# Two-block transformer on one core: 32-slot experts with contiguous weights, other key and output steps in the recurrence, a pre-normed half-step

## The chip, the cores and the metric

One core of one Trainium2 chip runs the whole program. The metric is the device time of one execution in microseconds (us), as the median of the runs. The engines go by the profile's short names: PE is TensorE's matmul (PEld its weight load), DVE is VectorE, ACT is ScalarE, POOL is GpSimd and SP is SyncE, which issues nearly all DMAs here.

## The reference

All is float32, batch 1, width 1024. The first block is a gated feed-forward half-step on 272 tokens, a hybrid attention mixer and a second half-step. The second block has two layers over 256 latent and 256 context tokens: layer 0 has a gMLP mixer, layer 1 a bidirectional recurrence, and each ends with a mixture of 32 experts, two per token (layer 0 on 512 tokens, layer 1 on the 256 latents).

```python
def swiglu(x, w_gate, w_up, w_down):
    return (jax.nn.silu(x @ w_gate) * (x @ w_up)) @ w_down

def _wkv_step(S, inp):                       # one token of the recurrence
    r_t, w_t, k_t, v_t, a_t, b_t = inp
    sa = jnp.einsum('zbhvk,zbhk->zbhv', S, a_t)
    S = S * w_t[..., None, :] + sa[..., :, None] * b_t[..., None, :] + v_t[..., :, None] * k_t[..., None, :]
    return S, jnp.einsum('zbhvk,zbhk->zbhv', S, r_t)

def hier_moe(h, ...):
    ...
    top_logit, top_idx = lax.top_k(exp_logits, TOP_K)           # 2 of the chosen group's experts
    weights = (p_grp * jax.nn.softmax(top_logit, axis=-1)).astype(h.dtype)
    ...
    def expert_block(args):
        xb, e = args
        return (jax.nn.silu(xb @ w_gate[e]) * (xb @ w_up[e])) @ w_down[e]
```

The context's recurrence only makes the state with which that of the latents starts, in both directions.

## The kernel before

Activations lie feature-major: 128 features on the partitions, eight chunks of them, tokens along the free axis. Nothing is kept in lower precision. A product that has to be exact is done by `mm3` (L1098) as three single-pass products of two-part operands; `wpart` (L1077) and `split` make the parts, the high one on ACT, the low one on DVE. Weights come through a ring of buffers of 2 MB (`wbuf`, `wtile`, `more_ring`); their DMAs all stand in SP's queue, in the order of their use. The order of the instructions on each engine is set by the framework's scheduler from the program's order and its own timing model, not by hand.

*First half-step* (`ffn`, L328). The squares of the input are summed over features by products with ones (L304) into `r`, 1/sqrt of the mean square. The products run on the input that is only scaled by the gain (L335); `r` is multiplied into both products as they leave PSUM (L350, L351). The modulation vectors of both layers are made beside (`ada`, L593: 32 stationary columns, four column groups of PE in turn), so that its 2 KB rows and the half-step's weights alternate in SP's queue.

*Experts* (`moe`, `experts`, L983). Assignments are sorted into 64 slots per expert; two experts make a pass of 128 slots, so there are 16 passes per layer. A pass loads two gate and two up tiles of 2 MB (`wtile`, L282) and two buffers of down weights, each from two DMAs of 1 MB (L1011). In PE's columns 0 to 63 one expert runs, in 64 to 127 the other:

```python
for b, p in ((0, pg), (1, pu)):
    for k in range(KD):
        for j in range(2):
            nc.tensor.matmul(p[64 * j:64 * j + 64], X[:, k, 64 * j:64 * j + 64], W[2 * b + j][:, k], start=(k == 0), ...
```

These are the records of L998; L1017 is the down product, L921 and L927 gather the next pass's tokens, L963 and L966 add a pass's result to the residual stream. In DRAM a weight's row of 512 or 1024 floats is what lies together: 2 KB of it go to one partition at a time. Assignments beyond the 64 slots would be done after the passes in a loop of extra blocks (`extra`), whose count SP and the other engines load from `xinfo` (L1033). Layer 1's ring has eight buffers: two from before the layer and six opened at its start.

*Recurrence* (`rwkv`). It runs as eight units of four heads, four of the context and then four of the latents, each in both directions z and in four chunks of 64 tokens. A unit has stages that are put beside those of its neighbours:
- `unit_keys` (L1308): decays (`ts` L1344 and L1346, their running sum L1348, exponentials `W` and `Wi` L1350, L1351), keys (L1358, L1359), receptances (L1362), removal vectors and added keys `BX` (L1366 to L1371), and their products (L1382, masked on the way out at L1383, L1386 and L1389);
- `unit_inverse` (L1558): a triangular inverse; its 16-token blocks are solved row by row by 30 small DVE operations that depend on each other (L1592, L1593);
- `unit_values`, then `unit_steps` (L1412): for each chunk T (L1447), U (L1458), the next state (L1473, L1478, with `hs` by POOL at L1466), and for the latents the output, in which a product with 128 rows (L1487) and one with 64 (L1488) alternate:

```python
for z in range(2):
    ...
    for mm in range(NM):
        for hh in range(2):
            mmul(p[o, cs], CL[mm][1][:, hh, z, s], HV[:, hh, mm * 2 + z], start=True, stop=False, ...)
            mmul(p[o, cs], un.LBr[half(z), mm * 2 + hh, s], UV[half(z), z, cs], start=False, stop=True, ...)
```

The functions that the change touches follow with the profile's line numbers.

## Time and profile before

| | us |
|---|---|
| median of 3 runs | 2869.97 (2868.59 to 2870.29) |
| span of the profiled execution | 2864.8 |
| difference to the median | 5.2 |
| PE busy | 2589.3 (90% of the span) |
| DVE busy | 1491.7 (52%) |
| ACT busy | 933.0 (33%) |
| POOL busy | 314.4 (11%) |
| DMA | 616.64 MB, mean 215 GB/s |

The page gives the profiled execution's span and no other time of it. The shares are averages over stages. In order of time these are the first half-step, the mixer and the second half-step, then gMLP, the experts of layer 0 (about 1057 to 1607 us), the recurrence's projections, its units (about 1772 to 2311) and layer 1's experts (to the end). In the lines of groups "busy" is the sum over the records of a group and "mean ns" the duration of one; matmuls overlap each other, so a group's busy time can be less than count times mean. An f32 matmul of this program leaves two records.

### The profile page before, as it was taken

What the parts mean: (1) busy time and instruction counts of PE and PEld (TensorE: products, weight loads), DVE (VectorE), ACT (ScalarE), POOL (GpSimd) and SP (SyncE); (2) the same over time, 40 slices, a digit from 0 to 9 for tenths busy, and PEclk for the clock granted to TensorE, in tenths of its full rate; (3) what the DMA queues carried; (4) which work ended last, traced back from release to release, by engine and by line L of the source; (5) the groups of instructions that cost most, each with busy time, mean ns of one, the idle gap of its engine ahead of it and who ended that gap; (6) DMA issues with size and microseconds to landing.
All of it is one profiled execution on the core that took longest, in us unless ns stands there. A gap on an engine that the chain in (4) does not pass through costs nothing. (4 is left out here: it accounts for less than half of the span.)

```text
span 2864.8 us, 43441 instructions
## 1 busy us (share of the span) xinstructions
PE 2589.3 (90%) x17524; PEld 1719.8 (60%) x17524; DVE 1491.7 (52%) x3267; ACT 933.0 (33%) x1686; POOL 314.4 (11%) x460
## 2 busy tenths in 40 slices
PE   8998999998999979999999597787799979999987
PEld 7986757997788744433333286666677744333332
DVE  5644855664564453443333686988975452222222
ACT  4433654543442231111110354554443222111111
POOL 0000100000100000000000212556552000000000
PEclk9999979999999989999999799887676879999999
DMA  8688801543222159999999333221111459999996
GB/s 282 239 318 288 288 15 54 212 171 128 99 89 88 45 194 384 370 363 365 362 367 364 103 114 115 64 69 40 35 45 27 136 203 387 386 387 387 386 386 254
DMA packets 339235, 616.64 MB, mean 215 GB/s; under 512 B 29059, under 2 KB 77779, under 8 KB 336467
## 3 DMA queue, kind: packets, MB, share of 16 engines
q1 hardware_dynamic: 337040, 609.66, 59.4%
q10 hardware_dynamic: 1926, 4.13, 0.4%
q8 instruction: 141, 2.31, 0.3%
q14 instruction: 64, 0.52, 0.1%
q0 software_dynamic: 64, 0.02, 0.0%
HBM read 604.15 MB, written 9.60 MB: 214 GB/s over the span
## 5 line engine op out<-in xcount | busy, mean ns | idle before, releaser
L998 PE MATMUL pg<-w,X 128*64 128x512 f32 x2048 | 510.1, 598 | 12.7 <-DMA w<-in_moe_up_dram 9.8
L1083 DVE TENSOR_TENSOR wl<-w,wh 128x1024 fp32r<-128x1024 f32 (+2 forms) x208 | 248.9, 1200 | 166.9 <-ACT wh L1082 165.1
L998 PEld LDWEIGHTS pg<-w,X 128*64 128x64 f32 x2048 | 154.0, 137 | 301.3 <-issue 281.8
L1082 ACT ACTIVATE wh<-w 128x1024 fp32r<-128x1024 f32 (+2 forms) x208 | 215.4, 1040 | 351.2 <-PE ps L1102 259.7
L966 DVE SCALAR_TENSOR_TENSOR Rl<-pc,mods,Rl 128x256 f32<-128x256 f32 x256 | 118.3, 480 | 298.0 <-PE pc L963 296.2
L1017 PE MATMUL py<-w,hT 128*64 128x512 f32 x992 | 231.6, 602 | 7.2 <-ACT hT L954 4.5
L1101 PE MATMUL ps<-xs,wh 128*128 128x272 f32 (+1 forms) x704 | 202.5, 288 | 3.5 <-ACT wh L1082 3.5
L1103 PE MATMUL ps<-xs,wl 128*128 128x272 f32 (+1 forms) x704 | 201.4, 288 | 1.4 <-DVE wl L1083 1.4
L1102 PE MATMUL ps<-xs,wh 128*128 128x272 f32 (+1 forms) x704 | 201.2, 286 | 0.0
L963 PE MATMUL pc<-tk,y 128*128 128x512 f32 (+1 forms) x512 | 139.6, 376 | 17.2 <-DVE Rl L966 8.0
L963 PEld LDWEIGHTS pc<-tk,y 128*128 128x128 f32 x512 | 77.6, 188 | 125.4 <-issue 72.9
L1017 PEld LDWEIGHTS py<-w,hT 128*64 128x64 f32 x992 | 67.4, 137 | 130.5 <-issue 115.1
L949 DVE SCALAR_TENSOR_TENSOR hh<-hh,tw,pg 128x512 f32<-128x512 f32 x32 | 23.9, 747 | 231.7 <-PE pg L998 231.7
L1101 PEld LDWEIGHTS ps<-xs,wh 128*128 128x128 f32 x704 | 134.0, 190 | 8.4 <-ACT wh L1082 4.7
L1103 PEld LDWEIGHTS ps<-xs,wl 128*128 128x128 f32 x704 | 133.4, 190 | 4.4 <-issue 2.5
L1102 PEld LDWEIGHTS ps<-xs,wh 128*128 128x128 f32 x704 | 133.8, 190 | 0.1
L976 ACT ACTIVATE y<-py 128x512 fp32r<-128x512 f32 x62 | 37.0, 597 | 279.1 <-PE py L1017 237.9
L977 DVE TENSOR_TENSOR y<-py,y 128x512 fp32r<-128x512 f32 x62 | 42.6, 687 | 136.8 <-ACT y L976 136.8
L928 ACT ACTIVATE X<-px 128x512 f32<-128x512 f32 x64 | 35.4, 596 | 228.0 <-PE pg L998 214.8
L948 ACT ACTIVATE hh<-pg 128x512 f32<-128x512 f32 x32 | 19.1, 598 | 254.6 <-PE pg L998 254.6
L1102 PE MATMUL ps<-hid,wh 128*128 128x272 f32 (+1 forms) x352 | 100.1, 284 | 0.0
L1103 PE MATMUL ps<-hid,wl 128*128 128x272 f32 (+1 forms) x352 | 100.0, 284 | 0.0
(492 smaller groups left out, 5528.7 us busy)
## 6 DMA issues: line engine op xcount, KB each, us to landing
w<-in_moe_gate_dram SPq DMA_DIRECT2D x64, 2048.0 KB, 9.4
w<-in_moe_up_dram SPq DMA_DIRECT2D x64, 2048.0 KB, 19.7
w<-in_moe_down_dram SPq DMA_DIRECT2D x128, 1024.0 KB, 14.4
w<-in_ada_w_dram SPq DMA_DIRECT2D x24, 2048.0 KB, 9.3
w<-in_w_down_dram SPq DMA_DIRECT2D x16, 1408.0 KB, 6.7
w<-in_w_gate_dram SPq DMA_DIRECT2D x8, 2048.0 KB, 9.0
w<-in_w_up_dram SPq DMA_DIRECT2D x8, 2048.0 KB, 7.8
w<-in_ga_w_in_dram SPq DMA_DIRECT2D x8, 2048.0 KB, 10.7
```

What stands on the lines that cost most here:

```text
L928: nc.scalar.activation(X[:, b * 4:(b + 1) * 4].rearrange("p k s -> p (k s)"), p[:, :4 * width], AF.Copy)
L963: nc.tensor.matmul(p[:, :n], y[j][:rows, k * 128:(k + 1) * 128], o, start=(j == 0), stop=(j == 1))
L966: nc.vector.scalar_tensor_tensor(R[t][:, k], p[:, s], self.mod(l, 5, k, t), R[t][:, k], op0=OP.mult, op1=OP.add)
L976: nc.scalar.activation(y[0][:rows, s], p[:rows], AF.Copy)
L977: nc.vector.tensor_tensor(y[1][:rows, s], p[:rows], y[0][:rows, s], op=OP.subtract)
L998: nc.tensor.matmul(p[64 * j:64 * j + 64], X[:, k, 64 * j:64 * j + 64], W[2 * b + j][:, k], start=(k == 0), stop=(k == KD - 1), skip_group_ ...
L1017: nc.tensor.matmul(p[64 * j:64 * j + 64], hT[:, k, 64 * j:64 * j + 64], Wd[b][:, j, k], start=(k == 0), stop=(k == 3), skip_group_check=True)
L1082: self.nc.scalar.activation(hi, view, AF.Copy)
L1083: self.nc.vector.tensor_tensor(lo, view, hi, op=OP.subtract)
L1101: mm(p, w[0], x[1], start=start, stop=False, skip_group_check=True)
L1102: mm(p, w[0], x[0], start=False, stop=False, skip_group_check=True)
L1103: mm(p, w[1], x[0], start=False, stop=stop, skip_group_check=True)
```

## The change

Eight things are changed together.
- The expert weights are laid out by the host so that a tile's part for one partition is contiguous: 16 KB for gate and up, 8 KB for down, which is loaded for two experts by one DMA of 2 MB.
- Layer 1 has 32 slots per expert, so four experts make a pass and there are eight passes; layer 0 keeps 64.
- Layer 1's six ring buffers are allocated after the layer's other tiles.
- `unit_keys` makes decays that start with a column of ones (`W1`, four tiles that live as long as the units), `Wi` for both halves of `BX` in one tile with a single buffer, and `BX` as (scaled ta on ACT) times key (DVE for the removal vectors, POOL for the added keys), then one product of 512 columns with `Wi`; the copies, `b0` and the separate addition of 1 on DVE are gone.
- `unit_inverse` does the row solve of every other unit on POOL.
- `unit_steps` issues the output products of the latents by shape.
- `ffn` norms the input of the first half-step before the products.
- The three parts of an exact product are issued small first in the first half-step and the mixer (as everywhere before), large first elsewhere. The router's logits take tokens as the stationary operand and come out token-major, without transposes.

```diff
-CAP = 64
-LIM = 64
+CAPS = (64, 32)
...
+LARGE_FIRST, SMALL_FIRST = ((0, 0), (0, 1), (1, 0)), ((0, 1), (0, 0), (1, 0))
...
-    for n in ("gate", "up", "down"):
-        a["moe_" + n] = f[f"moe_w_{n}_2"]
+    for n in ("gate", "up"):
+        a["moe_" + n] = f[f"moe_w_{n}_2"].reshape(2, NE, KD, 128, 512).transpose(0, 1, 3, 2, 4).reshape(2, NE, 128, 4096)
+    a["moe_down"] = f["moe_w_down_2"].reshape(2, NE, 4, 128, 2, 512).transpose(0, 1, 4, 3, 2, 5).reshape(2, NE, 2, 128, 2048)
...
-                nc.vector.tensor_scalar(x, h[:, k], self.v(g, k), None, op0=OP.mult)
+                if normed:
+                    nc.vector.scalar_tensor_tensor(x, h[:, k], self.v(g, k), r[:, :n], op0=OP.mult, op1=OP.mult)
+                else:
+                    nc.vector.tensor_scalar(x, h[:, k], self.v(g, k), None, op0=OP.mult)
...
+                    if normed:
+                        nc.scalar.activation(sg, pg[:, :n], AF.Silu)
+                        nc.vector.tensor_mul(sg, sg, pu[:, :n])
...
             pool = es.enter_context(self.tc.tile_pool(name=self.uid("moe"), bufs=1))
+            if l:
+                es.enter_context(self.more_ring(6, before=self.rings))
...
-                        nc.tensor.matmul(p[r, :SEQ], wr[:, k], h[:, k, t * SEQ:(t + 1) * SEQ], start=(k < 2), stop=(k >= KD - 2), skip_group_check=True)
-                    lp = rt.tile([128, SEQ], F32, tag="lp", name=self.uid("lp"), bufs=2)
-                    nc.scalar.activation(lp, p[:, :SEQ], AF.Copy)
...
+                        for j in range(2):
+                            c = t * SEQ + j * 128
+                            nc.tensor.matmul(p[j][:, :36], h[:, k, c:c + 128], wr[:, k, :36], start=(k == 0), stop=(k == KD - 1))
...
-                W = [self.wtile(s[2 * q + j], KD, 512) for s in (gate, up) for j in range(2)]
...
+                W = [[self.wtile(s[G * q + j], KD, 512) for j in range(G)] for s in (gate, up)]
+                for w, p in zip(W, (pg, pu)):
                     for k in range(KD):
...
+                        for j in range(G):
+                            a = slice(cap * j, cap * j + cap)
+                            nc.tensor.matmul(p[a], X[:, k, a], w[j][:, k], start=(k == 0), stop=(k == KD - 1), skip_group_check=True)
...
+                    for j in range(G * q, G * q + G, 2):
+                        t = self.wbuf()
+                        nc.sync.dma_start(t.rearrange("p (j x) -> p j x", j=2), down[j:j + 2, b].rearrange("j p x -> p j x"))
...
-        mm(p, w[0], x[1], start=start, stop=False, skip_group_check=True)
-        mm(p, w[0], x[0], start=False, stop=False, skip_group_check=True)
...
-                v.tensor_scalar(ts, ts, 1.0, None, op0=OP.add)
+                nc.scalar.activation(ts, ts, AF.Identity, bias=un.W1[z][:, 0, 0:1])
+
+                BX = un.BX[mm, z] = un.near("BX", [128, 4, 2, C], 4)
+                nc.scalar.activation(BX[:, :, z], un.chunks(ta), AF.Identity, bias=self.eps[:, 4:5], scale=-0.5)
+                nc.scalar.activation(BX[:, :, 1 - z], un.chunks(ta)[:, :, back], AF.Identity, bias=un.ka[:, 1, m:m + 1], scale=un.ka[:, 0, m:m + 1])
...
+                Wp, Wi = un.W1[z], un.near("Wi", [128, 4, 2, C], 1)
...
-                    v.tensor_mul(q[:, :, 1:], knv[o, :, 1:], Wv[o, :, :C - 1])
-                    v.tensor_copy(q[:, :, 0:1], knv[o, :, 0:1])
+                    v.tensor_mul(un.CL[mm][0][o, hh, z], knv[o], Wx[o])
...
-                v.scalar_tensor_tensor(b0, ta, 1.0, f(kn), op0=OP.add, op1=OP.mult)
-                v.scalar_tensor_tensor(BX[:, :, z], un.chunks(b0), -0.5, un.chunks(Wi), op0=OP.mult, op1=OP.mult)
...
-                g.tensor_tensor(t1, t1, f(k), op=OP.mult)
...
-                v.tensor_mul(BX[:, :, 1 - z], un.chunks(t1)[:, :, back], un.chunks(Wi)[:, :, back])
...
+                v.tensor_mul(BX[:, :, z], BX[:, :, z], knv)
+                g.tensor_tensor(BX[:, :, 1 - z], BX[:, :, 1 - z], un.chunks(k)[:, d], op=OP.mult)
...
+                v.tensor_mul(BX.rearrange("p c a t -> p (c a t)"), BX.rearrange("p c a t -> p (c a t)"), Wi.rearrange("p c a t -> p (c a t)"))
...
-                            mmul(p[o, cs], CL[mm][1][:, hh, z, s], HV[:, hh, mm * 2 + z], start=True, stop=False, skip_group_check=True)
-                            mmul(p[o, cs], un.LBr[half(z), mm * 2 + hh, s], UV[half(z), z, cs], start=False, stop=True, skip_group_check=True)
...
+                        for z in range(2):
+                            mmul(p[z][at[z][0], cs], CL[mm][1][:, hh, z, s], HV[:, hh, mm * 2 + z], start=mm + hh == 0, stop=False, skip_group_check=True)
+                for n in range(NM * 2):
+                    cs = slice(n * 64, (n + 1) * 64)
+                    for z in range(2):
+                        mmul(p[z][at[z][0], cs], un.LBr[half(z), n, s], UV[half(z), z, cs], start=False, stop=n == NM * 2 - 1, skip_group_check=True)
...
-            v.tensor_tensor(tv, Ls[:, s, s + 1:].unsqueeze(2).to_broadcast([128, n, s + 1]), Xs[:, s:s + 1, :s + 1].to_broadcast([128, n, s + 1]), op=OP.mult)
-            v.tensor_tensor(Xs[:, s + 1:, :s + 1], Xs[:, s + 1:, :s + 1], tv, op=OP.add)
...
+            e2.tensor_tensor(tv, Ls[:, s, s + 1:].unsqueeze(2).to_broadcast([128, n, s + 1]), Xs[:, s:s + 1, :s + 1].to_broadcast([128, n, s + 1]), op=OP.mult)
+            e2.tensor_tensor(Xs[:, s + 1:, :s + 1], Xs[:, s + 1:, :s + 1], tv, op=OP.add)
```

The order on three engines shows what the scheduler makes of it. The first place is PE in a step of the latents' units, the output products of one direction; `pt` is their PSUM tile, `HV` the state and the values, `UV` the step's result, `u` the unit's keys and receptances, `pi` and `pk` are products of a neighbouring unit. Before:

```order
L1487 MATMUL pt_17632<-HV_17555,u_16523 64x64
L1624 MATMUL pi_17953<-Xd_17813,LBc_17242 32x32 x22
L1382 MATMUL pk_18244<-u_18034,BX_18235 128x128 x4
L1382 MATMUL pk_18254<-u_18035,BX_18235 128x128 x4
L1473 MATMUL ph_17620<-UV_17586,u_16760 64x64 x2
L1488 MATMUL pt_17632<-UV_17586,u_16520 64x64
L1487 MATMUL pt_17632<-HV_17555,u_16523 64x64
L1488 MATMUL pt_17632<-UV_17586,u_16520 64x64
L1487 MATMUL pt_17632<-HV_17555,u_16525 64x64
L1488 MATMUL pt_17632<-UV_17586,u_16520 64x64
```

The changed program at the same step of the same unit, with line numbers of the changed file (L1506 is the product with 128 rows, L1510 that with 64):

```order
L1506 MATMUL pt_17481<-HV_17404,u_16396 64x64 x2
L1506 MATMUL pt_17481<-HV_17404,u_16398 64x64 x2
L1636 MATMUL pi_17733<-G_17664,XT_17663 32x32 x52
L1492 MATMUL ph_17469<-UV_17435,u_16621 64x64 x2
L1510 MATMUL pt_17481<-UV_17435,u_16393 64x64 x4
L1636 MATMUL pi_17733<-G_17664,XT_17663 32x32 x3
```

The program writes the two directions in turn, one tile each; the scheduler issues the four products of one shape and one tile together and those of the other direction later, as here in most steps.

The second place is the row solve of the seventh unit, which stands in POOL's queue in the changed program, with `hs` of a running unit's step (L1485) and the keys of the decayed values (L1425) in the same queue:

```order
L1614 TENSOR_TENSOR tp_18439<-Ls_18437,Xs_18438 128x55
L1615 TENSOR_TENSOR Xs_18438<-Xs_18438,tp_18439 128x5x11
L1447 COPY HV_18186<-Hst_13895 64x256 x2
L1614 TENSOR_TENSOR tp_18439<-Ls_18437,Xs_18438 128x48
L1485 TENSOR_TENSOR hs_18218<-HV_18186,WC_17105 64x2x64 x4
L1615 TENSOR_TENSOR Xs_18438<-Xs_18438,tp_18439 128x4x12
L1614 TENSOR_TENSOR tp_18439<-Ls_18437,Xs_18438 128x39
```

Before, all solves stood in DVE's queue, here between the keys of the next unit:

```order
L1366 SCALAR_TENSOR_TENSOR b_16726<-ta_16708,in_16645 128x256
L1592 TENSOR_TENSOR tp_16260<-Ls_16258,Xs_16259 128x28
L1593 TENSOR_TENSOR Xs_16259<-Xs_16259,tp_16260 128x14x2
L1358 TENSOR_TENSOR u_16522<-in_16530,W_16550 64x4x63
L1592 TENSOR_TENSOR tp_16260<-Ls_16258,Xs_16259 128x39
L1359 COPY u_16522<-in_16530 64x4
```

The third place is SP's queue at the start of layer 1; two gate loads stand further ahead in both. Before:

```order
L282 DMA w_20600<-in_moe_up_dram 128x8x512
L282 DMA w_20602<-in_moe_up_dram 128x8x512
L1011 DMA w_20688<-in_moe_down_dram 128x4x512 x2
L1011 DMA w_20691<-in_moe_down_dram 128x4x512 x2
L282 DMA w_20744<-in_moe_gate_dram 128x8x512
L282 DMA w_20746<-in_moe_gate_dram 128x8x512
L1033 TENSOR_LOAD xinfo
```

After:

```order
L286 DMA w_20429<-in_moe_gate_dram 128x4096
L286 DMA w_20431<-in_moe_gate_dram 128x4096
L286 DMA w_20433<-in_moe_up_dram 128x4096
L286 DMA w_20435<-in_moe_up_dram 128x4096
L286 DMA w_20437<-in_moe_up_dram 128x4096
L286 DMA w_20439<-in_moe_up_dram 128x4096
L1045 TENSOR_LOAD xinfo
L1022 DMA w_20557<-in_moe_down_dram 128x2x2048
```

The eight buffers hold the first pass's gate, up and down weights and the second pass's gates before, and the first pass's four gates and four ups now.

A fourth place is the start of the program on PE: the eight products with ones (L308 in the changed file) stand ahead of all products of the half-step, where before they alternated with them.

## Rows read from the trace of the kernel before

**Rows 1.** Windows of the two expert layers; columns: window, length, busy us (records) of PE, PEld, DVE, ACT, POOL, granted clock, DMA share, GB/s.
```profile
1100.00:1600.00 500.00, 482.96 (x2009) 194.27 (x2005) 187.61 (x471) 64.45 (x112) 0.00 (x0) 1.00 0.97 354
2400.00:2800.00 400.00, 370.41 (x1658) 149.08 (x1656) 107.44 (x283) 57.84 (x101) 0.00 (x0) 1.00 1.05 387
```

**Rows 2.** Waits of PE, window 2400 to 2860: us in total, times, longest us.
```profile
PE pg L998 <- DMA w<-in_moe_up_dram: 9.8, 7, 2.4
```

**Rows 3.** Windows of the recurrence's two stretches.
```profile
1772.00:2150.00 378.00, 296.17 (x4496) 244.94 (x4495) 328.95 (x777) 182.70 (x412) 213.26 (x331) 0.77 0.20 55
2150.00:2300.00 150.00, 137.44 (x1568) 107.17 (x1567) 70.68 (x156) 41.49 (x80) 23.24 (x45) 0.74 0.24 78
```

**Rows 4.** DMA issues of the page (count, KB each, us to landing), and the packet line.
```profile
DMA packets 339235, 616.64 MB, mean 215 GB/s; under 512 B 29059, under 2 KB 77779, under 8 KB 336467
...
w<-in_moe_gate_dram SPq DMA_DIRECT2D x64, 2048.0 KB, 9.4
w<-in_moe_down_dram SPq DMA_DIRECT2D x128, 1024.0 KB, 14.4
```

**Rows 5.** Windows of the first half-step: its first 50 us, and two of 2 us.
```profile
0.00:50.00 50.00, 40.02 (x256) 33.49 (x257) 24.28 (x49) 24.09 (x40) 1.27 (x7) 1.00 0.90 317
...
198.00:200.00 2.00, 2.00 (x19) 2.00 (x17) 0.00 (x0) 0.12 (x1) 0.00 (x0) 1.00 1.06 407
200.00:202.00 2.00, 2.00 (x19) 2.00 (x18) 1.03 (x1) 0.94 (x1) 0.00 (x0) 1.00 1.11 443
```

**Rows 6.** Timeline of PE, layer 1's first pass and its end: start us, us, operation, records.
```profile
2347.25 14.00 PE L998 MATMUL pg<-w,X 128*64 128x512 f32 x64
...
2838.52 3.65 PE L1017 MATMUL py<-w,hT 128*64 128x512 f32 x16 [0.75 <-ACT hT L954]
```

**Rows 7.** Lines of PE by form, window 100 to 260: busy us, mean ns, idle before.
```profile
L593 PE MATMUL pa<-w,cs 128*32 128x512 f32 x180 | 21.8, 599 | 1.2 <-DMA w<-in_ada_w_dram 1.2
```

**Rows 8.** Lines of DVE in the recurrence, window 1750 to 2310.
```profile
L1593 DVE TENSOR_TENSOR Xs<-Xs,tp 128x15 f32<-128x15 f32 (+7 forms) x120 | 36.5, 304 | 3.0
L1592 DVE TENSOR_TENSOR tp<-Ls,Xs 128x15 f32<-128x15 f32 (+7 forms) x120 | 33.9, 283 | 2.9
...
L1359 DVE COPY u<-in 64x4 f32<-64x4 f32 x64 | 22.1, 345 | 8.7 <-DMA in<-st 8.3
L1366 DVE SCALAR_TENSOR_TENSOR b<-ta,in 128x256 f32<-128x256 f32 x32 | 20.8, 649 | 0.3
L1367 DVE SCALAR_TENSOR_TENSOR BX<-b,Wi 128x256 f32<-128x256 f32 x32 | 18.7, 584 | 2.8 <-POOL kb L1406 2.3
L1371 DVE TENSOR_TENSOR BX<-t,Wi 128x256 f32<-128x256 f32 x32 | 17.6, 549 | 0.0
L1346 DVE TENSOR_SCALAR ts<-ts 128x256 f32<-128x256 f32 x32 | 13.2, 412 | 4.2 <-ACT ts L1344 4.0
L1383 DVE TENSOR_TENSOR LBc<-pk,cst 64x512 f32<-64x512 f32 x32 | 22.0, 688 | 4.4 <-PE pk L1382 3.7
```

**Rows 9.** Timelines of DVE and POOL near 1782 and 1814.
```profile
1781.93 0.42 DVE L1371 TENSOR_TENSOR BX<-t,Wi 128x256 f32<-128x256 f32 x1
...
1814.21 0.95 DVE L1371 TENSOR_TENSOR BX<-t,Wi 128x256 f32<-128x256 f32 x1
...
1813.06 1.81 POOL L1389 TENSOR_TENSOR u<-u,cst 64x256 f32<-64x256 f32 x2 [1.09 <-ACT u L1386]
```

**Rows 10.** Lines of PE in the recurrence, window 1750 to 2310.
```profile
L1488 PE MATMUL pt<-UV,u 64*64 64x64 f32 x256 | 50.9, 290 | 1.5 <-ACT UV L1459 1.5
L1487 PE MATMUL pt<-HV,u 128*64 128x64 f32 x256 | 49.5, 286 | 0.0
L1447 PE MATMUL pt<-HV,u 128*64 128x64 f32 x512 | 33.2, 274 | 5.9 <-DVE HV L1478 5.0 <-POOL u L1389 0.8
```

**Rows 11.** Timelines of DVE and PE at the program's start.
```profile
23.96 0.44 DVE L325 SCALAR_TENSOR_TENSOR rstd<-nw,rstd 128x272 f32<-128x272 f32 x1
...
13.26 0.60 PE L1101 MATMUL ps<-xs,wh 128*128 128x272 f32 x1 [1.06 <-ACT wh L1082]
```

174 lines of the change are left out of this document (86 added, 88 removed).

## The prediction

> **What bounds the kernel now.** I read the windows by stage first, then the waits, then the rows of each stage that the change touches. The two mixtures of experts take about 1,050 us of the span. In layer 0 (512 tokens) TensorE is busy 483.0 of 500 us at full clock while 354 GB/s arrive; in layer 1 (256 tokens) it is busy 370.4 of 400 us and the DMA engines deliver a flat 387 GB/s at a share of 1.05 [rows 1]. So layer 0 is bound by TensorE. Layer 1 is bound by the weight stream with TensorE close behind: TensorE's waits there are few, and the largest, 9.8 us, is for an up weight [rows 2]. The recurrence has two stretches [rows 3]: to 2150 us VectorE is busy 329.0 of 378 us, TensorE 296.2 and GpSimd 213.3, so VectorE leads but all three hand work to each other; from 2150 to 2300 TensorE is busy 137.4 of 150 us and nothing else is near. TensorE's clock is 0.77 and 0.74 of full there, against 1.00 in the expert layers.
>
> The sum is made against the one profiled execution: its span is 2864.8 us, 5.2 below the median of the runs, 2869.97. I add the 5.2 back at the end.
>
> **Contiguous and 32-slot experts.** A layer's weights are 64 gate and up tiles of 2048 KB and 64 down transfers of 1024 KB [rows 4] (the rows count both layers), that is 96 x 2.097 = 201.3 MB; eight tiles are on chip before layer 1 starts its products, so 184.5 MB stream at 0.387 MB/us: 477 us. Nearly all packets of before are the 2 KB rows of these weights (336467 of 339235 are under 8 KB [rows 4]). The nearest rows on longer packets are in the first half-step, where 2 KB rows (modulation weights) and 11 KB rows (down weights) take turns: 407 GB/s for the one, 443 for the other [rows 5], a ratio of 1.088. 387 x 1.088 = 421 GB/s, and 184.5 / 0.421 = 438 us: **-39 us**. Bounds: no faster (0), or 443 GB/s as in the short window (416 us, -61).
>
> The Trainium skill, page "DMA: Bandwidth & Descriptors", section "Where 436 GB/s comes from", speaks against this: for loads from HBM it says that the HBM side binds at about 358 GB/s per core. By that rule longer rows give nothing and the term is 0. The trace disagrees with the figure, since layer 1 already holds 387 for 400 us; it stays a rival below.
>
> TensorE must keep up. A pass of two experts now has 64 records in 14.00 us [rows 6], 219 ns each with two column halves; records with 32 stationary columns in four column groups take 21.8 / 180 = 121 ns [rows 7]. A pass of four experts has 128 + 64 records, 23.2 us, against 42.6 for two old passes (2 x 14.00 and 2 x 7.3, the output product's half being 3.65 [rows 6]). The 370.4 busy us of 400 are 60.3 per four experts (65.1 us of stream); the other 17.7 halve with the number of passes. That leaves 32 us of TensorE in 59.8 us of stream: layer 1 is bound by DMA. Layer 0 keeps its products and its TensorE bound: 0 (to -3).
>
> The end moves little: after the last landing one product of 3.65 us [rows 6] and the combine remain, as before; at half the clock they would cost some 4 more, and the earlier half product may now be over sooner, some 4 less: 0. The moved ring changes where six buffers lie, not that eight tiles are loaded while the tokens are routed, before the first product: 0, and if that cover shrank, 5 us for a tile that is late (2.097 MB at 0.421). In SP's queue the load of the overflow counts (xinfo) now stands ahead of the first pass's down weights instead of the second pass's up weights; the queue waits there for freed gate tiles in any case, so 0, and a microsecond for each that the counts would be later. One four-tile group is freed all at once, so the ring of eight is two groups: loads stop only if TensorE is a whole group (20 us) late.
>
> **Leaner keys and the solve on two engines.** VectorE loses [rows 8]: the copies 22.1, the keys' three products 20.8 + 18.7 + 17.6, the added one 13.2, and in half of the units the row solve, (36.5 + 33.9) / 2 = 35.2; in all 127.6. It gains 32 products of the short form (17.6) and 32 of 512 columns (22.0 as L1383 [rows 8]): 39.6. Net -88. But not all of it is VectorE's own. The product L1371 takes 0.42 us alone, and 0.95 when it meets two GpSimd operations of 0.9 [rows 9]. At 0.42 the three products are 40.3 instead of 57.1, so 17 of the 88 are waits for GpSimd that other instructions will inherit; and the solve, 8.8 us per unit on VectorE, goes to GpSimd, where a product of 64x256 takes 0.9 against 0.42 here, so at most 75 us come there, part of which blocks VectorE again. VectorE thus saves 46 to 88; I take 65, 57 of it in the first stretch.
>
> The Trainium skill, page "SBUF — State Buffer", names the cause: VectorE operations with two SBUF inputs and GpSimd operations share a port, and the second to start waits for the whole of the first. The rows agree. By that rule taken to the end the 35 us of the solve return as waits, and the recurrence is worth some 20 us less than I say.
>
> ScalarE gains three activations for each head pair and direction; it is busy 182.7 us of the first stretch's 378 [rows 3] and has room, but it stands in the steps' chain. GpSimd gains 40 to 88 us on its 213 (the solve at VectorE's price or at twice that, and the bonus' sums).
>
> **Grouped output products.** 512 records, 50.9 + 49.5 us, alternate between two shapes, about 200 ns each. The like product L1447, which is not interleaved with another shape, has 512 records in 33.2 us, 65 ns each, its outputs alternating between column halves [rows 10]. The order of the changed program shows that most runs are four of one shape into one half, so I take between one and two times L1447's price: 33 to 66 us in place of 100.4, -34 to -67, or 45, half in each stretch.
>
> First stretch: VectorE 329 - 57 at its present share (0.87) would end in 313 us, 65 sooner; TensorE (296 - 22 = 274) would then be busy 0.88 of it and GpSimd over 0.8, which three engines that wait for each other will not reach. At a share of 0.80 VectorE ends in 340: -38, rounded to -40. Second stretch: TensorE is the bound, 22 us less, of which the state's chain takes some: -17. **-57 us** for the recurrence; bounds -20 and -87 (-65 and -22).
>
> **The small edits.** The first half-step's products now need the norm, whose last instruction ends at 24.4, where the first product starts at 13.26 [rows 11]. In the order of the changed program the norm's eight sums stand ahead of all products, so it will be earlier than that. TensorE is busy only 40.0 of these 50 us while DMA has a share of 0.90 [rows 5], so weights set the pace and cover part of the delay: +2 (0 to +9). The PSUM multiplies that fall there lie beside a full TensorE: 0. The router's logits lose an activation, two transposes and an add per 256 tokens, at 0.4 us each, and get more, shorter matmuls: 0 (-3 to +2). The order of the three parts of a product changes no count: 0.
>
> **Sum.** 2864.8 - 39 - 57 + 2 = 2770.8; with the 5.2, **2776 us**. Its own range is 2750 to 2800.
>
> **Rivals.**
> A. The expert stream does not get faster, because 387 GB/s is what HBM or the engines give, or because TensorE, half idle, is granted its lower clock. For it: the flat 386 to 387, and the clock of 0.74 beside a TensorE that is 0.92 busy [rows 3]; at 1.2 GHz a pass would be 64 us against 59.8. Against it: 443 [rows 5], and a full TensorE at 1.00 [rows 1]. It gives 2870 - 57 + 2 = 2815.
> B. GpSimd takes the recurrence's place as the bound: its queue is in order, and the state's products wait behind the solve and the masks; Wi has one buffer, so ScalarE's next exponential waits for VectorE's product with the steps' copies behind it. Of the first stretch's 40 some 3 remain, of the second 17: 2870 - 39 - 20 + 2 = 2813.
> C. Both go fully: 443 GB/s (-61) and the recurrence -87: 2870 - 148 + 2 = 2724.
> D. Slower. Rows of 16 and 8 KB that start at multiples of 16 KB let the queues collide in HBM, and the rate falls. The farthest row for long packets is the program's start, 317 GB/s with the input's 8.5 KB rows among them [rows 5]. Then layer 0 turns DMA-bound too: 201.3 / 0.317 = 635 against 550 us, and layer 1 184.5 / 0.317 = 582 against 477: +190 - 55, or 3005. It decides below 385.8 / (550 + 477 + 55) = 357 GB/s. Against it: 443 with 11 KB rows, contiguous like these.
> E. The change does not do what it says: an expert of layer 1 with more than 32 assignments would run a serial block of some 20 us. From the reference's routing of these inputs the fullest has 26: no weight beyond what stands in D's chance.
>
> **The numbers.** Chances: forecast 0.56, A 0.14, B 0.15, C 0.11, D 0.04. The range takes A, B and C in: 2715 to 2828. A measurement of this kernel can tell about 0.2% (6 us) from no change. Only D is slower (0.04); A and B together are at 2852, and 0.01 is for what brings even that back to no change; faster 0.95.
>
> **What would show it.** Layer 1's windows at 415 to 430 GB/s with TensorE busy well under the whole, and its products in four column groups near 121 ns a record; layer 0's windows as before; the y products at 45 to 70 us in all; VectorE some 65 us less in the recurrence and no engine above 0.9 in its first stretch. Wrong would be: a layer 1 rate still at 387 (A) or under 357 (D); GpSimd over 0.85 with VectorE's products lengthened (B); a first half-step more than 9 us longer.

## The result, and the profile after

The changed kernel takes **2786.61 us** (median of six runs, 2781.13 to 2806.92); the kernel before, measured beside it again, 2870.13. The ratio is 0.9721 with a 95% interval of [0.968, 0.9763]: faster by 84 us. Ratios leave out runs more than 1.5% above the fastest of the same kernel (four of the thirteen of the kernel before that ran beside e0 to e3 below), so a ratio can differ a little from that of two medians. The forecast was 2776 us, in a range of 2715 to 2828.

The profiled execution of the changed kernel took 2806.92 us; its span is 2804.9. So against the span of before, 2864.8, the two traces show a difference of 59.9 us, not 84; the mixer, which is not changed, is 7 us longer in it, and the recurrence is at the upper end of what other executions of the same program take. That is why the stages are compared here, and not only the totals. A stage runs from the last instruction of the stage ahead to its own last one (a router to the first product of its experts), read from the two traces, in us:

| stage | before | after | difference | forecast |
|---|---|---|---|---|
| first half-step | 255.0 | 257.8 | +2.8 | +2 |
| mixer | 240.6 | 247.8 | +7.2 | 0 |
| second half-step and gMLP | 503.0 | 501.9 | -1.1 | 0 |
| router, layer 0 | 58.5 | 53.4 | -5.1 | 0 |
| experts, layer 0 | 551.4 | 550.9 | -0.5 | 0 |
| projections | 159.3 | 158.0 | -1.3 | 0 |
| recurrence | 543.4 | 534.3 | -9.1 | -57 |
| router, layer 1 | 36.1 | 32.5 | -3.6 | 0 |
| experts, layer 1 | 517.5 | 468.2 | -49.3 | -39 |

The windows of the changed kernel answer to [rows 1, 3, 5]; the columns are the same (busy us and records of PE, PEld, DVE, ACT and POOL, granted clock, DMA share, GB/s).

```profile
0.00:50.00 50.00, 34.83 (x216) 27.89 (x217) 20.34 (x39) 23.40 (x38) 1.27 (x7) 1.00 0.81 280
1100.00:1600.00 500.00, 483.63 (x2013) 194.46 (x2013) 189.13 (x479) 64.29 (x112) 0.00 (x0) 1.00 0.89 355
2400.00:2700.00 300.00, 201.72 (x1125) 59.03 (x1126) 39.08 (x97) 21.72 (x38) 0.00 (x0) 0.80 1.01 424
1775.00:2150.00 375.00, 282.31 (x4476) 232.90 (x4478) 273.69 (x526) 212.96 (x500) 250.11 (x447) 0.76 0.20 55
2150.00:2290.00 140.00, 118.36 (x1588) 100.17 (x1582) 71.90 (x153) 43.44 (x85) 30.26 (x53) 0.73 0.27 88
```

The third line is layer 1: 387 GB/s have become 424 [rows 1], and TensorE, busy 0.93 of the window before, is busy 0.67 of it. It now waits for weights again and again, where its largest wait of before was 9.8 us in all [rows 2]. From the waits of PE, window 2400 to 2760 (us in total, times, longest):

```profile
PE pg L1010 <- DMA w<-in_moe_gate_dram: 51.5, 21, 3.9
PE pg L1010 <- DMA w<-in_moe_up_dram: 48.2, 17, 3.9
```

The packets of the page, and the down loads, which are now one of 2 MB for two experts [rows 4]:

```profile
DMA packets 174364, 616.56 MB, mean 220 GB/s; under 512 B 28035, under 2 KB 76755, under 8 KB 138835
w<-in_moe_down_dram SPq DMA_DIRECT2D x64, 2048.0 KB, 12.4
```

And the timeline of PE: layer 1's first pass, four column groups of 32, against [rows 6]; 128 records in 13.94 us are 109 ns each. The last line is from the first half-step: the first product, which started at 13.26 before [rows 11].

```profile
2336.68 13.94 PE L1010 MATMUL pg<-w,X 128*32 128x512 f32 x128
23.50 0.82 PE L1116 MATMUL ps<-xs,wh 128*128 128x272 f32 x2 [6.00 <-DVE xs L1088]
```

Within layer 1 the 49.3 us divide by three moments of the stream of loads. From the first load that resumes to the last landing it was 481.3 us and is 438.0 (-43.3); the first load resumes 10.7 us after the first product before, 8.1 after (-2.6); from the last landing to the end it was 25.5 and is 22.1 (-3.4).

In the recurrence the parts fell as forecast and the stage did not. The lines of PE by form (1750 to 2305) show the output products at 28.4 + 28.2 us, against 49.5 + 50.9 [rows 10]:

```profile
L1506 PE MATMUL pt<-HV,u 128*64 128x64 f32 x256 | 28.4, 275 | 0.0
L1510 PE MATMUL pt<-UV,u 64*64 64x64 f32 x256 | 28.2, 276 | 0.2 <-ACT UV L1478 0.2
```

The lines of DVE by form there show what has taken the place of the products of [rows 8]:

```profile
L1381 DVE TENSOR_TENSOR u<-in,W 64x256 f32<-64x256 f32 x64 | 36.0, 563 | 0.7
...
L1394 DVE TENSOR_TENSOR BX<-BX,Wi 128x512 f32<-128x512 f32 x32 | 28.4, 888 | 3.7 <-POOL tp L1614 1.2 <-POOL BX L1386 1.1 <-POOL t L1393 1.0
...
L1385 DVE TENSOR_TENSOR BX<-BX,in 128x256 f32<-128x256 f32 x32 | 18.7, 586 | 7.4 <-ACT BX L1366 7.0
```

In the first stretch VectorE is busy 273.7 us where the forecast had 329 - 57 = 272, TensorE 282.3 (274), GpSimd 250.1 (213 + 40 = 253). Yet the stage is hardly shorter, and no engine is busy much over 0.75 of the stretch. What it waits for is the question of the experiments.

### The profile page after: what moved, and what is told of

Its sections match the earlier page's. It is cut to its first block, busy times and chain, and to the rows that moved or that the text cites. A ratio compares the mean times of both kernels' runs of the same rounds, so it can differ in the third digit from the quotient of the medians.

```text
span 2804.9 us, 42502 instructions
## 1 busy us (share of the span) xinstructions
PE 2409.0 (86%) x17278; PEld 1619.7 (58%) x17278; DVE 1354.4 (48%) x2792; ACT 926.2 (33%) x1715; POOL 358.5 (13%) x590
## 5 line engine op out<-in xcount | busy, mean ns | idle before, releaser
L1010 PE MATMUL pg<-w,X 128*64 128x512 f32 (+1 forms) x2048 | 451.1, 665 | 114.5 <-DMA w<-in_moe_gate_dram 58.8
L1010 PEld LDWEIGHTS pg<-w,X 128*64 128x64 f32 (+1 forms) x2048 | 116.9, 133 | 408.9 <-issue 240.7
L1116 PE MATMUL ps<-xs,wh 128*128 128x272 f32 (+1 forms) x1408 | 260.5, 286 | 7.3 <-DVE xs L1088 6.0
L1116 PEld LDWEIGHTS ps<-xs,wh 128*128 128x128 f32 x1408 | 219.0, 189 | 13.0 <-DVE xs L1088 7.6
L1030 PE MATMUL py<-w,hT 128*64 128x512 f32 (+1 forms) x976 | 179.7, 601 | 9.0 <-ACT hT L965 4.5
L977 DVE SCALAR_TENSOR_TENSOR Rl<-pc,mods,Rl 128x256 f32<-128x256 f32 x192 | 89.5, 480 | 179.2 <-PE pc L974 178.5
L974 PE MATMUL pc<-tk,y 128*128 128x512 f32 (+1 forms) x384 | 114.0, 397 | 18.6 <-ACT y L987 7.0
L1116 PE MATMUL ps<-hid,wh 128*128 128x272 f32 (+1 forms) x704 | 129.5, 284 | 0.0
L1116 PEld LDWEIGHTS ps<-hid,wh 128*128 128x128 f32 x704 | 108.9, 188 | 4.2 <-issue 4.2
L1030 PEld LDWEIGHTS py<-w,hT 128*64 128x64 f32 (+1 forms) x976 | 48.8, 124 | 104.9 <-issue 86.9
```

The source lines that it names most:

```text
L974: nc.tensor.matmul(p[:, :n], y[j][:rows, k * 128:(k + 1) * 128], o, start=(j == 0), stop=(j == 1))
L977: nc.vector.scalar_tensor_tensor(R[t][:, k], p[:, s], self.mod(l, 5, k, t), R[t][:, k], op0=OP.mult, op1=OP.add)
L1010: nc.tensor.matmul(p[a], X[:, k, a], w[j][:, k], start=(k == 0), stop=(k == KD - 1), skip_group_check=True)
L1030: nc.tensor.matmul(p[a], hT[:, k, a], Wd[b][j][:, k], start=(k == 0), stop=(k == 3), skip_group_check=True)
L1116: mm(p, w[a], x[b], start=start and n == 0, stop=stop and n == 2, skip_group_check=True)
```

## The experiments

Each kernel differs from the changed one by the edit shown. Ratios are to the kernel before, run beside it. Ahead of the single runs, the stages in which they differ, from their traces (us):

| kernel | median | ratio | mixer | recurrence | experts, layer 1 |
|---|---|---|---|---|---|
| before | 2870.13 | 1 | 240.6 | 543.4 | 517.5 |
| e11_before_again | 2868.05 | 0.998 [0.9941, 1.0019] | 230.3 | 553.8 | 517.5 |
| changed | 2786.61 | 0.9721 [0.968, 0.9763] | 247.8 | 534.3 | 468.2 |
| e0_again | 2805.46 | 0.9781 [0.9679, 0.9884] | 259.0 | 524.0 | 468.7 |
| e1_solve_on_dve | 2774.46 | 0.9676 [0.9588, 0.9764] | 241.9 | 504.1 | 470.7 |
| e2_rows_2k | 2833.50 | 0.9888 [0.9851, 0.9925] | 245.1 | 529.3 | 511.2 |
| e3_64_slots | 2842.18 | 0.9888 [0.9768, 1.0007] | 263.8 | 528.3 | 503.1 |
| e4_solve_all_pool | 2756.45 | 0.9581 [0.952, 0.9643] | 233.8 | 490.5 | 470.4 |
| e5_s_ungrouped | 2783.09 | 0.9649 [0.9588, 0.971] | 255.4 | 514.6 | 469.9 |
| e6_s_oldkeys | 2783.95 | 0.9703 [0.962, 0.9786] | 230.6 | 517.2 | 469.0 |
| e7_s_wi2 | 2770.89 | 0.9625 [0.9554, 0.9697] | 245.1 | 503.5 | 469.5 |
| e8_other_units | 2779.55 | 0.967 [0.9612, 0.9728] | 241.7 | 516.3 | 468.0 |
| e9_small_edits_undone | 2779.22 | 0.9657 [0.9601, 0.9713] | 250.2 | 508.8 | 470.8 |
| e10_all_pool_unnormed | 2754.47 | 0.9573 [0.953, 0.9616] | 240.4 | 499.7 | 468.4 |

### What repeats

The changed kernel and the one before, unchanged, on other chips.

> The changed kernel once more, for a second profile: the first was of an execution of 2806.9 us, while four of six took 2781 to 2788. If the difference lies in the clock of the mixer (granted 0.64 from 403 to 453 us, the stage 7 us longer than before), a profile near 2784 has the mixer some 7 to 10 us shorter and the expert layers unchanged within 3 us. If it lies in the recurrence, that stage (539 us to 2304) is shorter by 15 or more.

> The kernel before once more, for a second profile. If the mixer's and the recurrence's lengths follow the granted clock from execution to execution and not the change, the mixer here lies anywhere from 230 to 265 us (240.6 in the first profile, 234 to 264 in the changed kernels) and the recurrence within 12 us of 543; the other stages repeat within 1 us.

The execution of e0 that was profiled took 2809.8 us and not some 2784, so what was expected of a faster one was not put to the test. The median of e0 is 19 us above that of the first six runs, and its ratio, 0.9781, is worth some 63 us and not 84; the two intervals overlap, so the change's gain is known to some 20 us only.

Layer 1 repeats to 0.5 us in both kernels. The recurrence does not: 524.0 beside 534.3, and 553.8 beside 543.4. Two more kernels below (e2, e3) run the changed recurrence untouched and take 529.3 and 528.3. So its real gain is the mean of two, 548.6, less the mean of four, 529.0: **20 us**, with some 5 us of doubt on either mean. The mixer differs by up to 34 us between kernels that share its code (last section).

### Layer 1: the rows' length, or the slots

e2 loads the same tiles from the old layout, so in 2 KB rows; e3 keeps the new layout and gives layer 1 64 slots again.

```diff
-        gate, up, down = (i["moe_" + n][l] for n in ("gate", "up", "down"))
+        gate = i["moe_gate"][l].rearrange("e (k p) f -> e p k f", p=128)
...
+                        for jj in range(2):
+                            nc.sync.dma_start(t[:, jj], down[j + jj][:, :, b * 512:(b + 1) * 512])
```

> The changed kernel with the expert weights laid out as before (rows of 2 KB, down weights in 1 MB transfers), 32 slots kept. Theory (the rows' length makes the rate): layer 1's windows fall from 425 to about 387 GB/s and the whole is about 43 us longer (184.5 MB at the one and the other). Rival (eight passes instead of sixteen make the gain): rate and time as in the changed kernel within 8 us.

```diff
-CAPS = (64, 32)
+CAPS = (64, 64)
```

> The changed kernel with 64 slots in layer 1 too, contiguous rows kept. Theory (with longer rows alone TensorE bounds layer 1): its busy time of 60.3 us per four experts gives 482 us for the layer's products, 35 to 45 us longer than the changed kernel, at about 395 GB/s with TensorE over 0.97 busy. Rival (the rows alone carry the gain): within 8 us of the changed kernel at 415 GB/s or more.

Either part alone gives little: 511.2 us with the slots alone (-6), 503.1 with the long rows alone (-14), both together 468.2 (-49). The windows say why. e2 first (columns as above):

```profile
2400.00:2700.00 300.00, 191.52 (x1058) 57.14 (x1058) 39.27 (x97) 21.13 (x37) 0.00 (x0) 0.81 1.05 387
```

Its rate is that of before to the last digit, whatever TensorE does: 387 GB/s belongs to the 2 KB rows. The size of the transfers, which e2 changes back for the down weights, is not the cause: in each 10 us of that window e2 has 385 to 388 GB/s, whether gate and up weights (2 MB each) or down weights (1 MB) are under way, and the changed kernel 414 to 435. And e3:

```profile
2400.00:2450.00 50.00, 49.87 (x240) 21.44 (x238) 15.82 (x46) 8.74 (x15) 0.00 (x0) 1.00 1.01 424
...
2650.00:2700.00 50.00, 47.86 (x216) 18.62 (x214) 12.54 (x30) 5.76 (x10) 0.00 (x0) 1.00 0.96 397
```

It starts at the full 424 GB/s and sags to 397, because TensorE, busy 0.96 at its full clock, no longer frees the buffers in time. SP's queue shows that wait (us in total, times, longest):

```profile
SPq L286 <- PE pg L1010: 105.8, 19, 11.5
```

Two bounds lay some per cent apart: with its old rows the layer takes 511.2 us (e2), with its old products 503.1 (e3), so lifting one met the other.

### The recurrence: where the solve stands

e1 keeps all eight solves on VectorE; e4 puts all on GpSimd; e8 swaps which units go where (and puts the ring of layer 1 back).

```diff
-                            self.unit_inverse(units[n - 1], (v, nc.gpsimd)[n % 2])
+                            self.unit_inverse(units[n - 1], v)
```

> The changed kernel with every unit's row solve on VectorE. Theory (the solve on GpSimd holds up the steps: for the third unit it lasts from 1885.8 to 1951.0 us there between masks and state products, 10 us on VectorE for the fourth): the recurrence is 20 to 45 us shorter, VectorE some 35 us busier in it. Rival (the chain of the steps bounds the stage whatever engine solves): within 8 us. Second rival (VectorE needs the relief): longer by 10 to 30.

```diff
-                            self.unit_inverse(units[n - 1], (v, nc.gpsimd)[n % 2])
+                            self.unit_inverse(units[n - 1], nc.gpsimd)
...
-                    self.unit_inverse(units[-1], v)
+                    self.unit_inverse(units[-1], nc.gpsimd)
```

> The changed kernel with every unit's row solve on GpSimd. Theory (a solve in GpSimd's queue lasts some 65 us where VectorE takes 10, and the steps wait for it): with eight in place of four the recurrence is longer than in the changed kernel (524 to 534 us) by another 20 to 60. Rival (only the third unit's solve, at the change from context to steps, hurt): longer by under 10.

```diff
-                            self.unit_inverse(units[n - 1], (v, nc.gpsimd)[n % 2])
+                            self.unit_inverse(units[n - 1], (nc.gpsimd, v)[n % 2])
...
-                    self.unit_inverse(units[-1], v)
+                    self.unit_inverse(units[-1], nc.gpsimd)
```

> The changed kernel with the other four units' solves on GpSimd (second, fourth, sixth, eighth in place of first, third, fifth, seventh), and layer 1's ring allocated ahead of the layer's tiles as before. Theory (a solve on GpSimd costs time only where its 30 operations are queued among the masks and state products of a running unit, as with the third and fifth unit; with all eight there the recurrence took 490 us, on VectorE 504, in the changed kernel 524 to 534): the time goes with the longest solves, not with how many GpSimd does; a recurrence of 490 to 515 us if no solve lasts over 50 us, 520 or more if two do. Rival (alternating the engines is itself bad): 520 to 535 whatever the solves last. The ring: routing and layer 1 after it within 3 us of the changed kernel (32.5 and 468).

After e1 it looked settled: 504.1 us with the solves back on VectorE, 25 less than the mean of the changed recurrence. (e7 and e9 below, whose solves are on VectorE too, have 503.5 and 508.8.) My theory was that the solve does not belong on GpSimd, since its 30 operations depend on each other and stand in order behind other work. The timeline of POOL in the changed kernel shows this for the third unit (start us, us):

```profile
1885.83 0.66 POOL L1614 TENSOR_TENSOR tp<-Ls,Xs 128x15 f32<-128x15 f32 x1
1886.55 1.08 POOL L1660 MEMSET X<- 32x512 f32 x2
1887.71 0.23 POOL L1615 TENSOR_TENSOR Xs<-Xs,tp 128x15 f32<-128x15 f32 x1
...
1900.72 0.67 POOL L1615 TENSOR_TENSOR Xs<-Xs,tp 128x55 f32<-128x55 f32 x1
1901.47 1.74 POOL L1408 TENSOR_TENSOR u<-u,cst 64x256 f32<-64x256 f32 x2
1903.18 0.47 POOL L1614 TENSOR_TENSOR tp<-Ls,Xs 128x60 f32<-128x60 f32 x1
1903.61 1.03 POOL L1425 TENSOR_TENSOR kb<-BX,WC 128x512 f32<-128x512 f32 x1
...
1950.80 0.22 POOL L1615 TENSOR_TENSOR Xs<-Xs,tp 128x15 f32<-128x15 f32 x1
```

From first to last that is 65.2 us for 12.3 us of its own operations; masks (L1408), products (L1425) and fills stand between. On VectorE the fourth unit's solve takes 10.3 us (1961.3 to 1971.5). The third unit's inverse ends at 1975.9, and its steps wait for it: the timeline of ACT has their copies of T (L1468), the next one 49.1 us after the last.

```profile
1937.89 0.38 ACT L1468 ACTIVATE T<-pt 64x256 f32<-64x256 f32 x1 [0.88 <-PE pt L1466]
...
1974.67 1.21 ACT L1661 ACTIVATE X<-pi 32x512 f32<-32x512 f32 x2
...
1987.03 0.36 ACT L1468 ACTIVATE T<-pt 64x256 f32<-64x256 f32 x1
```

But with all eight on GpSimd (e4) the recurrence is the shortest of all, 490.5 us, and 499.7 in e10. These are single executions, but the medians of kernels that ran beside each other agree: e4 is 14 us under e7, e10 25 us under e9, of which e9's old logits are some 8. So the theory, as I had it, fell. The price of the operations is no ground for it either: the lines of e1 (DVE, 1750 to 2270) and of e4 (POOL, same stretch) are nearly equal, 74.9 us in all against 77.9.

```profile
L1615 DVE TENSOR_TENSOR Xs<-Xs,tp 128x15 f32<-128x15 f32 (+7 forms) x120 | 38.2, 318 | 3.1
L1614 DVE TENSOR_TENSOR tp<-Ls,Xs 128x15 f32<-128x15 f32 (+7 forms) x120 | 36.7, 306 | 3.1
```

```profile
L1615 POOL TENSOR_TENSOR Xs<-Xs,tp 128x15 f32<-128x15 f32 (+7 forms) x120 | 39.2, 327 | 7.3
L1614 POOL TENSOR_TENSOR tp<-Ls,Xs 128x15 f32<-128x15 f32 (+7 forms) x120 | 38.7, 322 | 21.6 <-DVE Ls L1608 8.2 <-DVE nw L327 6.7
```

What the move frees on VectorE is seen in the whole recurrence's windows, of e1 and of e4: 380.9 us busy against 324.1, 56.7 of the 74.9 that were moved. Of the 18 between them some 12 come back as longer instructions on VectorE, which are three lines in the main: L1381 and L1383 below, of e1 and then of e4, and the copy L1376 (6.0 and 9.1 us). Much of the rest is overlap: neighbouring records overlap, and busy time counts that once.

```profile
L1381 DVE TENSOR_TENSOR u<-in,W 64x256 f32<-64x256 f32 x64 | 35.8, 559 | 0.7
L1383 DVE TENSOR_TENSOR u<-in,W 64x256 f32<-64x256 f32 x32 | 17.7, 554 | 0.1
```

```profile
L1381 DVE TENSOR_TENSOR u<-in,W 64x256 f32<-64x256 f32 x64 | 40.3, 630 | 0.7
L1383 DVE TENSOR_TENSOR u<-in,W 64x256 f32<-64x256 f32 x32 | 21.9, 684 | 0.8 <-PE pt L1466 0.6
```

The windows of the two whole recurrences:

```profile
1765.00:2270.00 505.00, 405.14 (x6114) 338.89 (x6115) 380.85 (x817) 258.94 (x592) 245.75 (x395) 0.77 0.25 79
```

```profile
1763.00:2253.00 490.00, 388.34 (x6124) 324.12 (x6122) 324.11 (x577) 261.08 (x597) 314.19 (x620) 0.81 0.27 83
```

The Trainium skill, page "SBUF — State Buffer", section "🔬 SBUF: two separate sides", has VectorE and GpSimd lock each other out of a shared port for whole instructions. The longer products agree with that, and the size does not agree with the rule taken to its end: about a sixth of what was moved returns as longer instructions (12 of 74.9), not all of it.

e8 is between: 516.3 us, 13 less than the changed kernel's mean, though one of its solves takes 77.3 us in POOL's queue. So the longest solve does not order these kernels:

| kernel | solves on GpSimd | longest solve there | longest waits between steps (after the second) | recurrence |
|---|---|---|---|---|
| e4 | 8 | 58.1, 50.6 | 37.5, 24.8 | 490.5 |
| e10 | 8 | 73.1 | 42.2 | 499.7 |
| e1 | 0 | none | 20.2 | 504.1 |
| e8 | 4 | 77.3 | 48.0, 26.9 | 516.3 |
| changed | 4 | 65.2, 55.3 | 49.1, 33.2 | 529 (mean of four) |

Nor is every such wait lost. The context's four units take 190.8 us from the second step to the latents' first in the changed kernel, with the wait of 49.1 in it, and 193.7 in e1 without. The loss is in the latents, 213.7 to 221.8 against 190.2. Counted from the end of the projections, the changed kernel is 1 us ahead of e1 at the fifth unit's first step, 12 behind at the sixth's (in between is the solve of 55.3 us and the wait of 33.2), 19 at the seventh's and 32 at the eighth's. The first 12 us have a late solve beside them.

Of the other 20 some 8 go with TensorE's clock; for the rest I found no single wait. In the seventh unit's first step the changed kernel has a stretch in which TensorE is full. The same 432 records of the same program, from the changed kernel and from e0:

```profile
2186.71:2209.50 22.79, 22.43 (x432) 16.25 (x432) 10.50 (x23) 7.72 (x15) 2.70 (x6) 0.62 0.14 38
```

```profile
2198.76:2214.80 16.04, 15.62 (x432) 11.40 (x430) 10.70 (x23) 7.91 (x17) 2.70 (x6) 1.00 0.19 54
```

At a granted clock of 0.62 it takes 22.8 us, at 1.00 it takes 16.0; up to the sixth unit's first step the two executions agree within 0.3 us, and at the eighth's e0 is 24 us behind e1 and not 32. The latents' steps, first to last, of the changed kernel, e0, e1 and e4 (columns as above):

```profile
2058.93:2280.76 221.83, 183.65 (x2939) 154.75 (x2937) 133.60 (x277) 81.54 (x170) 82.12 (x157) 0.73 0.22 68
```

```profile
2071.42:2285.13 213.71, 175.34 (x2933) 148.61 (x2931) 133.47 (x277) 81.62 (x169) 81.42 (x157) 0.77 0.22 71
```

```profile
2055.40:2245.55 190.15, 168.39 (x2681) 141.16 (x2680) 127.04 (x276) 75.29 (x159) 72.51 (x121) 0.80 0.25 77
```

```profile
2039.15:2225.89 186.74, 154.96 (x2688) 130.32 (x2686) 118.08 (x217) 77.28 (x162) 94.43 (x194) 0.86 0.26 81
```

So the changed kernel has some 250 more TensorE records in this part, at a lower clock, and e4 has the records of e1 at a higher one. Whether the clock is a cause of these lengths or follows from the order of the work no run here parts.

### The recurrence: keys, products, Wi

Three kernels with all solves on VectorE, so to be set against e1. e5 has the output products alternate by shape as before; e6 has the keys of before; e7 gives Wi two buffers (and makes W1, two tiles of four chunks each, into one to find the room).

```diff
+                for z in range(2):
...
+                            mmul(p[o, cs], CL[mm][1][:, hh, z, s], HV[:, hh, mm * 2 + z], start=True, stop=False, skip_group_check=True)
+                            mmul(p[o, cs], un.LBr[half(z), mm * 2 + hh, s], UV[half(z), z, cs], start=False, stop=True, skip_group_check=True)
```

> The kernel with all solves on VectorE (recurrence 504 us, whole 2774), output products alternating between their two shapes as before. Theory (TensorE bounds the last 150 us): the products take 100 us again instead of 57 and the recurrence is 15 to 30 us longer. Rival (the steps' chain of copies between engines bounds it): under 8 us longer, TensorE merely busier.

```diff
-                BX = un.BX[mm, z] = un.near("BX", [128, 4, 2, C], 4)
-                nc.scalar.activation(BX[:, :, z], un.chunks(ta), AF.Identity, bias=self.eps[:, 4:5], scale=-0.5)
...
+                v.scalar_tensor_tensor(b0, ta, 1.0, f(kn), op0=OP.add, op1=OP.mult)
+                v.scalar_tensor_tensor(BX[:, :, z], un.chunks(b0), -0.5, un.chunks(Wi), op0=OP.mult, op1=OP.mult)
```

> The kernel with all solves on VectorE, with the keys' stage of before (its copies, additions and three products on VectorE, t1 times k on GpSimd, Wi with two buffers). Theory (VectorE bounds the first 380 us): 53 us more of VectorE make the recurrence 25 to 45 us longer. Rival (no engine bounds it, the chain does): 0 to 10 us longer. Second rival (the single Wi buffer and ScalarE's added work cost as much as VectorE gains): within 5 us or shorter.

```diff
-                Wp, Wi = un.W1[z], un.near("Wi", [128, 4, 2, C], 1)
+                Wp, Wi = un.W1[:, z], un.near("Wi", [128, 4, 2, C], 2)
```

> The kernel with all solves on VectorE, and two buffers for Wi instead of one. If ScalarE's exponentials wait for VectorE's product with Wi (9.3 us of waits in all in the changed kernel) and hold up the copies of the steps behind them, the recurrence is 5 to 15 us shorter; if not, within 4 us.

Both parts help, and not in sum. With the new keys alone the stage is 514.6 us (-34 from 548.6), with the grouped products alone 517.2 (-31), with both 504.1 (-44.5). Set against e1, e5 is 10.5 us longer and e6 13: each lies between what its theory and its rival had, so neither is borne out. The keys' gain is in the head, from the end of the projections to the second step, where no other unit's steps cover them: 112.9 and 115.8 us in the two traces of before, 111.5 in e6, 96 to 101 with the new keys (106 in e8). The products' gain can only be in the latents, the units with outputs: 199.2 us in e5, 190.2 in e1, so 9 of the 44 us by which the products became cheaper. But e9, which has the grouped products too, takes 198.7, so these 9 are not clear of what else differs between such kernels. Wi's single buffer costs nothing that shows (503.5 against 504.1).

### The small edits, and a shorter version

e9 has the solves on VectorE and puts back the first half-step's order, the logits and the order of the three parts. e10 is e4 with the first half-step put back.

```diff
-                self.ffn(h, T1, "g_ffn1", i["w1_gate"], i["w1_up"], i["w1_down"], beside, normed=True)
+                self.ffn(h, T1, "g_ffn1", i["w1_gate"], i["w1_up"], i["w1_down"], beside)
...
-            self.order = LARGE_FIRST
+            self.order = SMALL_FIRST
```

> The kernel with all solves on VectorE, with three small edits undone whose stages lie apart: the first half-step not normed ahead, the router's logits as before, the parts of every exact product small first. Theory: the first half-step ends at 255.0 us as before instead of 258; routing takes 58 and 36 us as before instead of 53.5 and 32.4 (logits); second half-step, gMLP and projections stay within 1 us (order of parts). Rival for the logits (their stage moves with the order in which the scheduler places the layer's first loads: 50.4 to 57.4 us in runs that share them): within 2 us of 53.5 and 32.4.

> The changed kernel with all solves on GpSimd and the first half-step not normed ahead: the two edits that gained, together. The recurrence stays at 490 us and the first half-step ends 3 us earlier: some 2753 us, 3 below the kernel with all solves on GpSimd; if the scheduler's order of the recurrence changes with it, up to 20 us off either way.

Put back, the first half-step takes 253.1 and 252.6 us, against 257.8 to 259.1 where it norms first: the edit **costs 5 to 6 us**. Its first product waits 6.00 us for the norm, which ends at 20.97 instead of 24.40.
The logits give some 5 us in layer 0. The stage as a whole is 58.5 to 60.2 us with the old ones and 53.4 to 53.6 in most kernels with the new, but 50.4 to 57.4 in all that share them, since the tokens `h` are ready earlier or later and a record of the products takes 0.41 us or 0.28. From the last write of `h` to the last logit (`lg`) it is 10.2 us before and 10.3 in e9, 5.2 in the changed kernel and in e6, 3.0 in e2. In layer 1 the stage is 32.4 us with the old ones (e9) against 32.3 in e1, so nothing. The order of parts is worth 1.4 us in the projections (159.4 against 158.0), nothing measurable elsewhere. The place of the ring (e8) moves the router and the experts of layer 1 together by no more than 3 us.
e10 and e4, which noise does not part, are the best versions here: e10 has 2754.47 us, 0.9573 [0.953, 0.9616] of before, 32 us under the changed kernel.

## Why the prediction was right, and which of its steps failed

The time came out 10.6 us above the forecast and inside its narrower range, but partly by luck: a recurrence that gave far less than forecast was made up for by layer 1, the routers and other stages that gave more.

- **The expert stream, -39 forecast, -49.3 measured.** The mechanism held: 424 GB/s (forecast 421), TensorE at 0.67, layer 0 unchanged. The stream itself gave 43.3 of it; at 424 in place of 421, 438.0 us as forecast, but the old stream was 481.3 and not 477. The two ends, which I set at 0, gave 2.6 and 3.4. Records took 109 ns, not 121. The ratio of 1.088 was read off two windows of 2 us; that it came this close to the 1.096 of the whole layer is luck too.
- **One reading of the packets was wrong** and changed nothing: 201.3 MB in rows of 2 KB are 98,304 packets a layer, so the experts' rows are 196,608 of the 339,235, six in ten and not nearly all.
- **Rival A fell**: the rate belongs to the length of the rows (e2). The Trainium skill, page "DMA: Bandwidth & Descriptors", section "Where 436 GB/s comes from", has the HBM side bind at about 358 GB/s per core; the measured 424, with one core running, decides against it. The table under "Measured" on the same page of the Trainium skill has 425 GB/s for one transfer of 16 MB that GpSimd issues; the rate here, of loads that SP issues, agrees with that.
- **The slots' part in that term** I costed only as the condition "TensorE must keep up". e3 shows how much hung on it: 35 of the 49 us.
- **The recurrence, -57 forecast, about -20 measured (from -9 to -30 by the pair of executions).** This is the step that failed, and in it the sentence "At a share of 0.80 VectorE ends in 340". The busy times of the first stretch were right within 9 us; over the whole recurrence VectorE gave 53 (405.4 to 352.6) and not 65, inside the bounds of 46 to 88. The share was a choice without a row: measured are 273.7 of 375 us, 0.73, and with TensorE at 0.75 and GpSimd at 0.67 no engine's busy time bounds that stretch; that the hand-overs between them do is the likely reading, which no run isolates. Of the second stretch's -17 the grouped products give 9 at most that could be seen (e5 against e1), and e9 leaves even that in doubt.
- **Rival B was half right.** Its price was the measured one (recurrence -20), and its first half is seen: steps wait up to 49.1 us for a solve in POOL's queue, and the changed kernel's recurrence is 25 us longer than that of e1, though not every such wait is lost time. Its second half, Wi, is wrong (e7). And its condition, that GpSimd becomes the bound, is wrong: it is busy 0.67, and with twice the solves (e4) the stage is shorter.
- **The price of the solve on GpSimd**, bounded between VectorE's price and twice that, is VectorE's.
- **The small edits.** First half-step +2 forecast, +3 in the traces of before and after, 5 to 6 when undone alone. Logits 0 (-3 to +2) forecast, about -5 measured, outside its bounds: the chain there is serial. What was removed behind the last product (transposes, activation, add) gives 1.7 us of it, 1.9 to 0.2 from its end to the last logit; the rest is that the products end sooner after the last `h`, 5.0 us and not 8.3. The router of layer 1 is 3.6 us shorter, which I can't put to any one edit; it varies from 32.3 to 35.4 between kernels that share it.
- **The sum**: -49 - 20 - 5 - 4 - 3 + 3 = -78 by stages, the mixer left out, against -84 in the medians (-63 in those of e0), with two stages that differ by 10 us and more from execution to execution.

**What stays open**: why all solves on GpSimd give 490 to 500 us, all on VectorE 504 to 509, and half of them 516 to 534. VectorE is freed by 57 us in e4, the order that the program takes on every engine differs between these kernels, and so does the clock that TensorE is granted in the latents' steps (0.73 to 0.77 in the changed kernel, 0.80 in e1, 0.86 in e4 and e10), so the runs don't part the three.

## What to carry to other kernels

Where two resources stand within some per cent of each other, cost an edit together with the one that lifts the other: here -6 and -14 alone, -49 together. Busy time that is saved in a stretch that no engine fills is not yet time: here 53 us of VectorE and 44 of products gave 20. Find the part that nothing covers (here the head of the recurrence) and count the saving there. A chain of small dependent operations that moves to another engine's queue lasts as long as what stands between its links, 65 us for 12 of work, whatever its price; whether that is lost depends on what waits for it. Here a mixture of two engines was worse than either alone.

## What the runs showed of the hardware that was not expected

The mixer runs the same instructions in all these kernels, and takes 230 to 264 us. It follows the clock that TensorE is granted: from e11 and from e3, the same 1307 records in windows that hold the mixer,

```profile
254.00:484.00 230.00, 209.25 (x1307) 150.52 (x1307) 152.80 (x407) 127.23 (x279) 17.20 (x26) 0.96 0.41 142
```

```profile
259.00:522.00 263.00, 241.03 (x1307) 167.00 (x1307) 152.81 (x405) 127.33 (x278) 17.14 (x26) 0.82 0.35 124
```

with 0.93, 0.89 and 0.86 giving 234, 240 and 248 us in e4, before and after. The engine is busy 0.91 to 0.92 of the stage in both; why one execution is granted more of the 2.4 GHz than another no run here tells. The whole time goes with it: of the thirteen runs of the kernel before beside e0 to e3, the shortest, 2842.8 us, had a mean granted clock of 0.936 and the longest, 2892.0, of 0.914, and the others lie nearly in that order between. In layer 1 of the changed kernel, where TensorE waits for weights, the granted clock is 0.80 (a mean over both levels), and that costs nothing since the stream is the bound. And a 128-partition GpSimd operation of 15 to 64 elements took 325 ns on average, one on VectorE 312: for such small ones GpSimd was no slower.
